# All low halves and block differences of an MLP's input and up-projection on VectorE

## The chip, the cores and the metric

The kernel runs on one core of a Trainium2 chip. The metric is device time in microseconds (us): the median of several executions. A profile of one further execution shows each engine's instructions: TensorE (PE, with its weight loads as PEld), VectorE (DVE), ScalarE (ACT), GpSimd (POOL) and SyncE (SP), which issues most DMAs.

## The reference

Two layers of a transformer-like backbone over 1024 latent and 256 context tokens of width 1024. Each layer normalises and modulates its input, runs three token mixers side by side (Fourier, mLSTM, attention), projects and adds, and then runs a squared-ReLU MLP. The change touches only the MLP's first half, and the place where the second layer's input is made:

```python
def sqrelu_mlp(h, w_up, w_down):
    return jnp.square(jax.nn.relu(h @ w_up)) @ w_down

for l in range(DEPTH):
    mod = (jax.nn.silu(c) @ w_mod[l] + b_mod[l])[:, None, :]
    sh1, sc1, ga1, sh2, sc2, ga2 = jnp.split(mod, 6, axis=-1)
    h = modulate(rmsnorm(x, g_norm1[l]), sh1, sc1)
    ...   # the three mixers
    x = x + ga1 * (jnp.concatenate([y_f, y_m, y_a], axis=-1) @ w_out[l])
    x = x + ga2 * sqrelu_mlp(modulate(rmsnorm(x, g_norm2[l]), sh2, sc2), w_up[l], w_down[l])
    ...   # in the first layer the same for the context tokens
```

`w_up` is 1024x4096 and all data are float32.

## The kernel before

**Numbers in two halves.** A float32 product is made from three TensorE passes: every operand is split into a high half, which ScalarE writes by a rounding copy (L147), and a low half, the source minus the high half (L148). The low half is a subtraction of two operands in SBUF, and VectorE or GpSimd makes it. `mm3` (L134 to L144) then issues high times high, high times low and low times high.

**Who makes the low half** is set by short patterns. `lo_` steps through a pattern's letters with one counter for all patterns of a layer (G is GpSimd, V is VectorE):

```python
def lo_(pat, c=[0]):
    c[0] += 1
    return G if pat[c[0] % len(pat)] == "G" else V
```

`LF` is for the low halves of the MLP's input and, at the end of the first layer, of the second layer's input; `UL` for those of the up-projection's weights; `UA` for the additions and subtractions on those weights (L1262); `FA` for those on the input (L1351); `DA` and `DL` for the down-projection.

**The up-projection** is a 2x2 block product after Strassen and Winograd, with seven products in place of eight. The latent input, 1024 tokens by 1024 channels, is cut in four; its block sums and differences S1 to S4 are made once for a layer (L1351 and the `split` calls around it). I call that stretch the build: it begins with the eight scalings L1190 of the second token block, which wait for that block's norm, and takes both token blocks in turn. The weights come as 16 pairs of column groups. For each pair, `up_pair` makes four differences (L1262), splits up to eight weight blocks, runs the products and adds up the results from PSUM (L1295 and L1313 to L1326). The first pairs' two products that need only the first token block (three pairs in the first layer, eight in the second) run during the build, so that TensorE has something to do. Split weight blocks (tiles `c` and `x`) have eight places in turn.

**Beside it, in the first layer,** VectorE computes the modulation of the second layer: 192 multiply-and-sum instructions (L235), each on a 256 KB piece of `w_mt`, two for each piece. The pieces land in three buffers (`wf`), which also hold results on their way to memory.

**The order of the work** on each engine is fixed when the program is built: a scheduler goes through the instructions with a cost of its own for each and writes one list for each engine, which that engine then works through strictly in order. Where another engine makes an instruction, the lists come out otherwise.

Of the kernel before, what the change touches and what calls it, by code (L numbers as in the profile page):

```python
# [29 lines left out]
PK0 = (1, 2, 4, 5, 7)  # L30
PK1 = (4, 5, 6)
PO = (7, 4, 0, 1, 5, 2, 3, 6)
UA = "GGV"
UL = "GGV"
FA = "V"
LF = "GV"
DA = "V"
DL = "VVVG"
RQ = "MAAV"
# [24 lines left out]
def build(tc, A, out, dbg=None):  # L64
# [81 lines left out]
    def split(dst, src, hi=None, lo=None):  # L146
        (hi or S).activation(dst[0], src, AF.Copy) if (hi is None or hi is S) else hi.tensor_copy(dst[0], src)  # L147
        (lo or G).tensor_tensor(dst[1], src, f32(dst[0]), ALU.subtract)  # L148
# [279 lines left out]
    for l in range(2):  # L428
# [752 lines left out]
# [4 lines that stand above are left out]
        def raw(l_, i_, b, h=None, R=None):  # L1185
            n, w = BLK[b][1:]
            R = rstd_bcast(ss[b], n, D, wk, pst, "t") if R is None else R
            for k in (0, 4, 1, 5, 2, 6, 3, 7):
                x = xT[b][:, k]
                hk["raw"] = V.scalar_tensor_tensor(x, x, Gm[l_][i_][:, w, k:k + 1], R[:, :n], ALU.mult, ALU.mult)  # L1190
                sh = modT[l_][:, w, 24 * i_ + k:24 * i_ + k + 1]
                S.activation(x, x, AF.Identity, bias=sh)
                if h is not None:
                    split((h[:, 0, k], h[:, 1, k]), x, lo=lo_(LF))
                yield k

        def form(b):
            h = h_tile(b)
            for k in raw(l, 1, b):
                split((h[:, 0, k], h[:, 1, k]), xT[b][:, k], lo=lo_(LF))  # L1200
            return h
# [27 lines left out]
        def rtile():  # L1229
            i = nslot[1] = (nslot[1] + 1) % len(rslot)  # L1230
            return T(wk, [128, 1024], tag="r2") if rslot[i] is None else rslot[i]

        def csplit(src, pat, c=None):
            c = ctile() if c is None else c
            split((c[:, 0], c[:, 1]), src, lo=lo_(pat))
            return c

        def prod(ps, c, h, first, last, n=512):
            for k in range(4):
                sl = slice(128 * k, 128 * k + 128)  # L1240
                mm3(ps, c[:, 0, sl], c[:, 1, sl], h[k][0][:, :n], h[k][1][:, :n], first and k == 0, last and k == 3)
# [11 lines left out]
        def P_(tag="p"):  # L1253
            return T(*((wk, [128, 512]) if tag == "p" else (ring, [128, 512])), tag=tag)
# [6 lines left out]
        def up_pair(p, a, b):  # L1261
            add = lambda *x: lo_(UA).tensor_tensor(*x)  # L1262
            ra = rtile()
# [13 lines left out]
            def pr_(c, h):  # L1277
                ps = mmt()
                prod(ps, c, H[h], True, True)
                return ps  # L1280

            if a:
                c11 = csplit(B11, UL)
                ps = pr_(c11, "A11")
# [4 lines left out]
                if cxa:  # L1289
                    psc = mmt()  # L1290
                    prod(psc[:, :256], c11, cx[:4], True, False, 256)
                c21 = csplit(B21, UL)
                ps = pr_(c21, "A12")
# [3 lines left out]
                if cxa:  # L1297
                    prod(psc[:, :256], c21, cx[4:], False, True, 256)
                    c12 = csplit(B12, UL)
            if b and not a and ctx_all:  # L1300
                p1s[p] = P_()
                nc.sync.dma_start(p1s[p], dp1[p])
            if b or cxa:
                c22 = csplit(B22, UL)
            if b:
# [3 lines left out]
                add(B22, B22, B11, ALU.subtract)  # L1309
                ps = pr_(csplit(B22, UL), "S2")  # L1310
                tg = "p"
                u2 = P_(tg)
                V.tensor_tensor(u2, ps, p1s[p], ALU.add)  # L1313
                add(B21, B21, B22, ALU.subtract)
                ps = pr_(csplit(B12, UL), "S3")
                u3 = P_(tg)
# [29 lines left out]
        for k in raw(l, 1, 1):  # L1346
# [4 lines left out]
            add = lambda *x: lo_(FA).tensor_tensor(*x)  # L1351
            split(H["A22"][i], r22, lo=lo_(LF))
            add(r22, r21, r22, ALU.add)
            add(r21, r11, r21, ALU.subtract)
            add(r11, r22, r11, ALU.subtract)
            split(H["S2"][i], r11, lo=lo_(LF))
            add(r12, r12, r11, ALU.subtract)
            split(H["S3"][i], r21, lo=lo_(LF))
            split(H["S1"][i], r22, lo=lo_(LF))
            split(H["S4"][i], r12, lo=lo_(LF))  # L1360
# [341 lines left out]
```

## Time and profile before

| | before |
|---|---|
| median of 3 executions | 3067.19 us (3059.11 to 3071.19) |
| the profiled execution | 3061.46 us, span 3059.7 us |
| TensorE busy | 2848.2 us, 93% |
| VectorE busy | 2012.7 us, 66% |
| ScalarE busy | 1177.9 us, 38% |
| GpSimd busy | 1062.4 us, 35% |
| mean granted TensorE clock | 0.955 |

The span runs from the first to the last instruction; the profiled execution's own time is 1.8 us longer. Busy shares are means over stages with different limits, so the windows, one for each stage, say more: the builds lie near 820 to 901 us and 2357 to 2438 us, the steady parts of the up-projections near 908 to 1257 us and 2440 to 2694 us, and the passage from the first layer to the second near 1640 to 1760 us.

### The profile page before, as it was taken

How to read it: one execution, taken by the hardware profiler on the slowest of the kernel's cores; microseconds unless marked ns; L12 is line 12 of the kernel's file. 1: busy time of each engine (PE TensorE's matmuls, PEld its weight loads, DVE VectorE, ACT ScalarE, POOL GpSimd, SP SyncE). 2: the span in 40 equal slices, each digit the busy share in tenths (PEclk: the TensorE clock that was granted, in tenths of full speed). 3: DMA queues.
4: the chain of work that ended last, by engine and by line, in shares of the span. 5: the costliest groups of instructions: out<-in, count | busy, mean ns of one | idle time of the engine just before them, and what ended most of it. 6: DMA issues, size and time to landing. Idle time of an engine off the chain costs nothing.

```text
span 3059.7 us, 40746 instructions
## 1 busy us (share of the span) xinstructions
PE 2848.2 (93%) x14320; PEld 2344.3 (77%) x14320; DVE 2012.7 (66%) x3742; ACT 1177.9 (38%) x2283; POOL 1062.4 (35%) x945
## 2 busy tenths in 40 slices
PE   7998998999989999999999999898999899989996
PEld 6887866657768888888887787876767688868885
DVE  7769568642488767777787527457633854478887
ACT  3322244443343333233344432244433543434444
POOL 4212234111364444221225333233123665513334
PEclk7999999999989999999999999899999899999998
DMA  6514576223335544732121212465134343353321
GB/s 238 161 56 136 145 170 165 72 88 112 111 128 196 168 159 156 281 111 94 58 90 38 109 40 87 123 152 138 55 115 140 117 153 106 110 196 97 106 88 55
DMA packets 277872, 376.45 MB, mean 123 GB/s; under 512 B 63396, under 2 KB 154468, under 8 KB 276004
## 3 DMA queue, kind: packets, MB, share of 16 engines
q1 hardware_dynamic: 274788, 366.51, 38.4%
q0 software_dynamic: 576, 4.20, 0.4%
q10 hardware_dynamic: 2304, 3.15, 0.3%
q8 instruction: 113, 1.85, 0.3%
q14 instruction: 91, 0.75, 0.1%
HBM read 283.74 MB, written 90.02 MB: 122 GB/s over the span
## 4 chain that ended last, share of the span: by engine, by line
PE 61%; DVE 18%; DMA 8%; issue 6%; POOL 3%; ACT 2%; SPq 0%; DVEq 0%; POOLq 0%; ACTq 0%
PE mm L138 10%; PE mm L143 8%; PE mm L144 8%; PE v L1141 4%; PE mm L135 4%; PE mm L136 4%; PE mm L134 3%; DVE ac L677 2%; DVE A L148 2%; DVE junk L235 2%; PE mm L1466 2%; PE mm L140 2%; PE mm L141 2%; PE t L1466 2%; DMA gt<-in_w_mt 2%
## 5 line engine op out<-in xcount | busy, mean ns | idle before, releaser
L138 PE MATMUL mm<-A,wr 128*128 128x512 f32 (+1 forms) x840 | 315.1, 378 | 18.6 <-ACT rb L673 9.8
L135 PE MATMUL mm<-A 128*128 128x512 f32 (+1 forms) x654 | 251.1, 389 | 13.6 <-DVE A L148 11.3
L136 PE MATMUL mm<-A 128*128 128x512 f32 (+1 forms) x654 | 242.8, 387 | 0.3 <-DVE A L148 0.3
L134 PE MATMUL mm<-A 128*128 128x512 f32 (+1 forms) x654 | 237.3, 387 | 5.7 <-ACT A L147 5.7
L148 POOL TENSOR_TENSOR wr<-wf,wr 128x512 fp32r<-128x512 f32 x88 | 123.1, 1407 | 246.3 <-ACT wr L147 235.3
L143 PE MATMUL mm<-A,wr 128*128 128x512 f32 (+1 forms) x520 | 194.5, 375 | 7.9 <-DVE A L148 4.3
L138 PEld LDWEIGHTS mm<-A,wr 128*128 128x128 f32 x840 | 162.4, 194 | 49.8 <-ACT rb L673 11.3
L1141 PE MATMUL v<-PT,Vt 128*97 128x512 f32 (+1 forms) x336 | 180.4, 622 | 14.0 <-ACT PT L1140 13.6
L144 PE MATMUL mm<-A,wr 128*128 128x512 f32 (+1 forms) x520 | 193.2, 372 | 0.0
L138 PE MATMUL mm<-A,c 128*128 128x512 f32 (+1 forms) x520 | 184.4, 356 | 5.8 <-ACT c L147 3.6
L143 PE MATMUL mm<-A,c 128*128 128x512 f32 (+1 forms) x520 | 184.9, 356 | 3.3 <-DVE A L148 2.5
L144 PE MATMUL mm<-A,c 128*128 128x512 f32 (+1 forms) x520 | 183.9, 354 | 1.2 <-DVE c L148 1.2
L235 DVE SCALAR_TENSOR_TENSOR junk<-wf,t 128x512 bf16<-128x512 f32 x192 | 131.3, 684 | 67.7 <-DMA wf<-in_w_mt 64.1
L147 ACT ACTIVATE A<-wr 128x512 fp32r<-128x512 f32 x188 | 114.2, 625 | 148.3 <-PE mm L135 59.2
L147 ACT ACTIVATE A<-A 128x512 fp32r<-128x512 f32 x174 | 106.9, 625 | 158.5 <-PE mm L135 86.0
L148 DVE TENSOR_TENSOR A<-wr,A 128x512 fp32r<-128x512 f32 x146 | 131.0, 909 | 43.4 <-ACT A L147 29.0
L1140 ACT ACTIVATE PT<-s 128x512 f32<-128x512 f32 (+1 forms) x168 | 97.6, 583 | 159.2 <-PE s L144 157.4
L135 PEld LDWEIGHTS mm<-A 128*128 128x128 f32 x654 | 123.4, 189 | 42.5 <-DVE A L148 15.0
L134 PEld LDWEIGHTS mm<-A 128*128 128x128 f32 x654 | 122.7, 188 | 31.1 <-ACT A L147 6.9
L136 PEld LDWEIGHTS mm<-A 128*128 128x128 f32 x654 | 123.6, 189 | 24.8 <-DVE A L148 0.7
L138 PE MATMUL mm<-wr,A 128*128 128x256 f32 x464 | 134.1, 289 | 6.9 <-ACT rb L673 4.7
L148 POOL TENSOR_TENSOR A<-wr,A 128x512 fp32r<-128x512 f32 x42 | 75.8, 1809 | 177.9 <-ACT A L147 149.8
(504 smaller groups left out, 8274.0 us busy)
## 6 DMA issues: line engine op xcount, KB each, us to landing
wf<-in_w_mt SPq DMA_DIRECT2D x96, 256.0 KB
x<-in_w_up SPq DMA_DIRECT2D x40, 512.0 KB
r<-in_w_up SPq DMA_DIRECT2D x38, 512.0 KB
wr<-in_w_dn SPq DMA_DIRECT2D x36, 512.0 KB
gt<-in_w_mt SPq DMA_DIRECT2D x64, 256.0 KB
da<-wf SPq DMA_DIRECT2D x64, 256.0 KB
da<-p SPq DMA_DIRECT2D x64, 256.0 KB
wf<-in_w_in SPq DMA_DIRECT2D x56, 256.0 KB
```

Of the source, the lines that this page charges most:

```text
L134: PE.matmul(ps, lh, rh, start=first, stop=False, skip_group_check=True)
L135: PE.matmul(ps, lh, rl, start=False, stop=False, skip_group_check=True)
L136: PE.matmul(ps, ll, rh, start=False, stop=last, skip_group_check=True)
L138: PE.matmul(ps, lh, rh, start=first, stop=False)
L143: PE.matmul(ps, lh, rl, start=False, stop=False)
L144: PE.matmul(ps, ll, rh, start=False, stop=last)
L147: (hi or S).activation(dst[0], src, AF.Copy) if (hi is None or hi is S) else hi.tensor_copy(dst[0], src)
L148: (lo or G).tensor_tensor(dst[1], src, f32(dst[0]), ALU.subtract)
L235: V.scalar_tensor_tensor(junk, f, 1.0, cb[w], ALU.mult, ALU.mult, accum_out=(ga, modT[l])[kh][:, w, j:j + 1])
L1140: S.activation(PT[:, :nq], ps[:, :nq], AF.Exp, scale=scale)
L1141: PE.matmul(po[:97, :nq], Vt[kt // 2][:, kt % 2, h % 2], PT[:, :nq], start=i == 0, stop=i == len(kts) - 1)
L1466: PE.matmul(o, blk[f"B{h + 1}{q + 1}"][k][:, 128 * jj:128 * jj + 128], f[:, k, 256 * h:256 * h + 256], start=h + k == 0, stop=h * k == 3)
```

## The change

Three patterns lose their G, so that every instruction under them goes to VectorE. `FA` had none.

```diff
-UA = "GGV"
-UL = "GGV"
+UA = "V"
+UL = "V"
 FA = "V"
-LF = "GV"
+LF = "V"
 DA = "V"
 DL = "VVVG"
```

What is computed is the same. The lists of the engines change. On VectorE, in the middle of the first layer's build, before: `x_` are the blocks being added and subtracted, `A_` and `wr_` the low halves of S1 to S4, `c_` those of weights, `wf_` results.

```order
L1351 TENSOR_TENSOR x_1563_7126<-x_1563_7126 128x512
L148 TENSOR_TENSOR wr_8026<-x_1563_7126,wr_8026 128x512
L1351 TENSOR_TENSOR x_1563_7126<-x_1563_7126 128x512
L1351 TENSOR_TENSOR x_1479_6740<-x_1563_7126,x_1479_6740 128x512
L148 TENSOR_TENSOR A_1674_8025<-x_1479_6740,A_1674_8025 128x512
L1251 SCALAR_TENSOR_TENSOR wf_8180<-mm_8104,wf_8180 128x512
```

The same place in VectorE's list after the change:

```order
L1351 TENSOR_TENSOR x_1563_7126<-x_1563_7126 128x512
L148 TENSOR_TENSOR c_8289<-r_1705_8222,c_8289 128x512
L148 TENSOR_TENSOR wr_8026<-x_1563_7126,wr_8026 128x512
L1351 TENSOR_TENSOR x_1479_6740<-x_1479_6740 128x512
L148 TENSOR_TENSOR wr_8030<-x_1563_7126,wr_8030 128x512
L1251 SCALAR_TENSOR_TENSOR wf_8180<-mm_8104,wf_8180 128x512
```

The low halves `c_8289` and `wr_8030`, which stood in GpSimd's list, now stand between VectorE's differences.

In the steady part of the first layer's up-projection, one stretch of VectorE's list before: `junk_` are the products for the modulation, each pair with its piece `wf_`, and `x_1716` the low half of a weight block.

```order
L1251 SCALAR_TENSOR_TENSOR wf_9916<-mm_9745,wf_9916 128x512
L235 SCALAR_TENSOR_TENSOR junk_9922,ga_8449<-wf_9920,t_8450 128x512
L235 SCALAR_TENSOR_TENSOR junk_9924,ga_8449<-wf_9920,t_8455 128x512
L148 TENSOR_TENSOR x_1716_8341<-r_2049_10196,x_1716_8341 128x512
L235 SCALAR_TENSOR_TENSOR junk_9938,mod_7_67<-wf_9936,t_9926 128x512
L235 SCALAR_TENSOR_TENSOR junk_9940,mod_7_67<-wf_9936,t_9931 128x512
L235 SCALAR_TENSOR_TENSOR junk_9944,mod_7_67<-wf_9942,t_9926 128x512
```

From the same result `wf_9916` on, after:

```order
L1251 SCALAR_TENSOR_TENSOR wf_9916<-mm_9745,wf_9916 128x512
L148 TENSOR_TENSOR c_10230<-r_2049_10196,c_10230 128x512
L235 SCALAR_TENSOR_TENSOR junk_9922,ga_8449<-wf_9920,t_8450 128x512
L235 SCALAR_TENSOR_TENSOR junk_9924,ga_8449<-wf_9920,t_8455 128x512
L1313 TENSOR_TENSOR p_10063<-mm_10050,p_9977 128x512
L148 TENSOR_TENSOR c_10263<-r_2050_10198,c_10263 128x512
L1262 TENSOR_TENSOR r_2050_10198<-r_2050_10198 128x512
L1317 TENSOR_TENSOR p_10081<-mm_10068,p_10063 128x512
L148 TENSOR_TENSOR x_1716_8341<-r_2050_10198,x_1716_8341 128x512
L1318 TENSOR_TENSOR p_10063<-mm_10031,p_10063 128x512
L235 SCALAR_TENSOR_TENSOR junk_9938,mod_7_67<-wf_9936,t_9926 128x512
```

Between the products on piece `wf_9920` and those on `wf_9936` there stood one low half; now there stand the sums of the next pair, two low halves and a difference.

## Rows read from the trace of the kernel before

**Rows 1.** The page: engine busy us (share of the span) xinstructions

```profile
PE 2848.2 (93%) x14320; PEld 2344.3 (77%) x14320; DVE 2012.7 (66%) x3742; ACT 1177.9 (38%) x2283; POOL 1062.4 (35%) x945
```

**Rows 2.** Windows: stretch and its length, busy us (xinstructions), clock, DMA

```profile
core 0: us, PE busy (x) PEld busy (x) DVE busy (x) ACT busy (x) POOL busy (x), PEclk, DMA share, GB/s
819.00:856.00 37.00, 29.71 (x147) 25.47 (x147) 28.16 (x58) 23.09 (x46) 17.45 (x16) 0.91 0.35 114
856.00:901.00 45.00, 32.40 (x174) 26.16 (x172) 44.93 (x44) 24.67 (x44) 30.78 (x20) 0.85 0.34 111
908.00:1257.00 349.00, 347.36 (x1815) 297.53 (x1814) 263.06 (x591) 120.82 (x209) 150.35 (x112) 1.00 0.53 172
...
2390.30:2437.70 47.40, 33.52 (x127) 24.60 (x126) 47.37 (x49) 27.35 (x49) 30.70 (x19) 0.82 0.33 111
2440.00:2694.00 254.00, 254.00 (x1090) 204.66 (x1089) 123.38 (x170) 100.39 (x165) 135.38 (x100) 1.00 0.37 124
```

**Rows 3.** TensorE's waits, 819 to 905 us: us in total, times, longest

```profile
PE mm L144 <- DVE c L148: 5.7, 2, 5.4
PE t L201 <- DVE rb_y L187: 4.8, 1, 4.8
```

**Rows 4.** TensorE's waits, 2350 to 2450 us

```profile
PE mm L138 <- ACT s L147: 8.4, 1, 8.4
```

**Rows 5.** Windows, TensorE alone, at the ends of the builds

```profile
880.00:905.00 25.00, 13.86 (x41) 0.66 0.40 137
2410.00:2438.00 28.00, 14.12 (x44) 0.70 0.38 131
2420.00:2430.00 10.00, 1.25 (x3) 0.50 0.20 59
```

**Rows 6.** VectorE in order of time, first build: start, us, instruction

```profile
855.89 5.35 DVE L1190 SCALAR_TENSOR_TENSOR x<-x,G,t 128x512 f32<-128x512 f32 x8
...
861.87 1.67 DVE L1351 TENSOR_TENSOR x<-x 128x512 f32<-128x512 f32 x1
863.47 0.68 DVE L1295 TENSOR_TENSOR wf<-mm,p 128x512 f32<-128x512 f32 x1
...
866.50 1.79 DVE L148 TENSOR_TENSOR A<-x,A 128x512 fp32r<-128x512 f32 x1
```

**Rows 7.** GpSimd in order of time, the same moments

```profile
861.53 1.47 POOL L148 TENSOR_TENSOR c<-r,c 128x512 fp32r<-128x512 f32 x1 [4.38 <-ACT c L147]
862.95 1.75 POOL L148 TENSOR_TENSOR A<-x,A 128x512 fp32r<-128x512 f32 x1
865.98 1.76 POOL L148 TENSOR_TENSOR A<-x,A 128x512 fp32r<-128x512 f32 x1 [1.27 <-DVE x L1351]
...
902.19 4.36 POOL L1262 TENSOR_TENSOR x<-x 128x512 f32<-128x512 f32 x3
906.50 1.28 POOL L148 TENSOR_TENSOR c<-x,c 128x512 fp32r<-128x512 f32 x1
```

**Rows 8.** VectorE in order of time, steady part of the first layer

```profile
1012.98 0.69 DVE L1318 TENSOR_TENSOR p<-mm,p 128x512 f32<-128x512 f32 x1
1013.59 0.69 DVE L148 TENSOR_TENSOR x<-r,x 128x512 fp32r<-128x512 f32 x1
1014.20 0.68 DVE L1320 TENSOR_TENSOR p<-mm,p 128x512 f32<-128x512 f32 x1
```

**Rows 9.** Windows, GpSimd's instructions of line L148 alone

```profile
819.00:856.00 37.00, 13.67 (x13) 0.91 0.35 114
856.00:901.00 45.00, 26.26 (x17) 0.85 0.34 111
```

**Rows 10.** VectorE by line, 908 to 1257 us: busy us, mean ns

```profile
L1251 DVE SCALAR_TENSOR_TENSOR wf<-wf 128x512 f32<-128x512 f32 x13 | 14.8, 1136 | 0.7 <-ACT wf L1250 0.7
L148 DVE TENSOR_TENSOR x<-x,x 128x512 fp32r<-128x512 f32 x18 | 13.6, 756 | 0.7 <-ACT x L147 0.7
L1248 DVE SCALAR_TENSOR_TENSOR p<-p 128x512 f32<-128x512 f32 x15 | 11.8, 784 | 0.0
...
L148 DVE TENSOR_TENSOR c<-x,c 128x512 fp32r<-128x512 f32 x9 | 7.4, 820 | 9.8 <-ACT c L147 9.8
```

**Rows 11.** VectorE's waits, 901 to 1258 us: us in total, times, longest

```profile
DVE junk L235 <- DMA wf<-in_w_mt: 64.1, 38, 4.1
```

**Rows 12.** Window: from the first layer to the second

```profile
1640.00:1720.00 80.00, 67.82 (x282) 53.31 (x281) 66.95 (x103) 46.12 (x90) 37.71 (x31) 0.91 0.22 85
```

**Rows 13.** TensorE's longest wait, 1640 to 1760 us

```profile
PE t L134 <- DVE x L1190: 4.0, 1, 4.0
```

## What is expected of the change

> **What bounds the kernel now.** I read the busy shares of the page first, then the stages by windows, then who ended TensorE's waits, then VectorE's and GpSimd's instructions in order of time. The shares say TensorE: 93% busy against VectorE's 66% and GpSimd's 35% [rows 1]. That is an average, so the windows decide. In the long middle of both up-projections TensorE never pauses: 347.4 of 349 us in the first layer, 254 of 254 in the second [rows 2]. What VectorE or GpSimd do there costs nothing as long as they keep ahead. In the stretch where the block differences of the MLP's input are made it is the reverse: VectorE is busy 44.9 of 45 us in the first layer and 47.4 of 47.4 in the second, while TensorE has 32.4 and 33.5 us of work [rows 2]. The waits agree: the longest of TensorE in the first layer is 5.4 us for a low half that VectorE makes, after 4.8 us for a norm chain on VectorE [rows 3]; in the second it is 8.4 us for ScalarE's copy of the last difference, which VectorE makes late [rows 4]. At the end of each stretch TensorE also runs slowly: 41 matmuls in 25 us at a granted clock of 0.66, 44 in 28 us at 0.70, of which 10 us at 0.50, that is 1.2 GHz, after it had stood idle [rows 5].
>
> **The change, part by part.** By the order, 292 subtractions leave GpSimd (950 instructions before, 658 after) and the same 292 stand on VectorE (3408, then 3700). The counts of the other engines are unchanged; TensorE's order shifts a little in the MLPs. The down-projection keeps its choices, because one counter serves all patterns and is still advanced once for each subtraction.
>
> Price of one moved subtraction: on VectorE undisturbed, neighbouring 128x512 subtractions start 0.60 us apart (1012.98, 1013.59, 1014.20) [rows 8]; on GpSimd one takes 1.3 us when it is alone and up to 1.8 in the build [rows 7]. But a GpSimd one isn't free for VectorE. The difference at 861.87 us and the low half at 866.50 us, both with two operands in SBUF, take 1.67 and 1.79 us beside GpSimd's subtractions, while the addition at 863.47, one operand of which is in PSUM, takes 0.68 us in the middle of one [rows 6, 7]. So a collision costs VectorE about 1.1 us, and the moved instruction 0.6.
> The Trainium skill, "SBUF — State Buffer", section "Who interferes with whom", says that a VectorE instruction with two SBUF inputs and a GpSimd one that reads SBUF take turns on a shared interface, the later one waiting for the whole of the other. The rows above agree, the PSUM case included. If every one of the 20 collided for 1.1 us, taking them away would give back 22 us for 12 spent, 10 us in that stretch, as an estimate from that rule; I go by the sum below instead.
>
> *The two build stretches.* First layer, 856 to 901 us: 44 VectorE and 20 GpSimd instructions, 17 of the latter low halves [rows 2, 9]; all 20 move. After: 64 x 0.60 us, and 0.06 us more for each of the eight scalings (eight take 5.35 us [rows 6]), is 38.9 us against 45.0: 6.1 us less. Second layer, 2390.3 to 2437.7 us: 49 and 19 instructions, 68 x 0.60 + 0.5 = 41.3 against 47.4: 6.1 us less. Together 12.2 us, if VectorE keeps never waiting. In the new order each low half stands close behind its difference, so a few will wait for ScalarE's high half (ScalarE is busy 24.7 and 27.4 us here [rows 2]); and in the second layer the last difference stands only a few places from the end, so that TensorE's 8.4 us wait shrinks less than the whole. I take 10 us of the 12.2. Bounds: nothing, if the waits for ScalarE eat it, and 12.2 plus what the clock gives back: 85 matmuls are busy 28.0 us [rows 5], at the undisturbed 254.0/1090 = 0.233 us [rows 2] it were 19.8, so 8.2 us more.
>
> *Before the first build, 819 to 856 us.* 13 low halves move [rows 9] onto an engine with 28.2 of 37 us busy [rows 2], part of that stretched by collisions; 13 x 0.60 = 7.8 fits into the 8.8 left. Nothing, between 4.8 us gained (the wait for the norm chain [rows 3] gone) and 4.8 lost (it doubles).
>
> *The steady up-projection, first layer.* 112 instructions move in 349 us [rows 2]. VectorE then has 263.1 + 112 x 0.60 = 330.3 us, less the collisions that end. These show in four groups as the excess over 0.69 us: 13 x 0.45, 18 x 0.07, 15 x 0.10, 9 x 0.13, 9.8 us [rows 10]. So 320.5 us, 92% of the stretch, with 28.5 us left. Queued there too are the products for the next layer's modulation (L235), 192 of them, in front of which VectorE stands 64.1 us waiting for their weights to land [rows 11]. If these waits stayed whole, 320.5 + 64.1 would be 35.6 us more than 349, and TensorE would pay that. I expect them to be filled: they come where VectorE goes through these products one behind the other with nothing else queued. In the order before, 114 of the 192 follow directly on another; in the order after 46, since the low halves now stand between. By that proportion 64.1 x 46/114 = 25.9 us of waiting remain, less than the 28.5. Cost: 0, between 0 and 35.6.
>
> *The steady up-projection, second layer.* 123.4 + 100 x 0.60 = 183.4 of 254 us [rows 2], without those products: 0. Some 70 us of VectorE's time stay idle there, so that what comes late is caught up.
>
> *From the first layer to the second, 1640 to 1720 us.* VectorE is busy 67.0 of 80 us and TensorE waits 4.0 us for its scalings [rows 12, 13]. Eight low halves move there and four just behind, all after that wait; at 0.6 us or less each that is under 5 us more on VectorE, and GpSimd keeps its share of the down-projection, so collisions go on. 0, within 3 us either way.
>
> **Sum.** The profiled execution took 3061.5 us, 3059.7 of it span. 10 us less is 3051.5. It stands 5.7 us under the median of 3067.2, so the forecast in the median's terms is 3057 us.
>
> **Rivals.** *More than the forecast:* the builds give all: 12.2 us, the clock's 8.2 and the norm chain's 4.8, 25 us, so 3042 us. For it: VectorE had no gap in either stretch [rows 2], and the slow matmuls stand right behind the idle time. Against: TensorE's order still begins the first full weight block with the product that needs the last differences, so some idle time stays, and with it some low clock.
> *Slower: VectorE becomes the bound in the first layer's steady stretch.* Low halves stand behind a product whose weights have not landed; the three buffers of these weights are also those in which results wait for their way out, and each is now held longer, since its two products no longer stand together. It decides as soon as more than 28.5 of the 64.1 us remain. With all of it: 35.6 less the builds' 10, 25.6 us more, so 3093 us. For it: 92% load and an engine that works strictly in order. Against: eight split weight blocks have room, each the work of 12 matmuls, 2.8 us at 0.233, so that a wait of 4.1 us (the longest [rows 11]) can pass unseen; and the fewer neighbours counted above.
> The Trainium skill, "Perfetto Trace Analysis", section "Optimizing Scalar/DVE Operations", would have work taken off VectorE when it is saturated, to GpSimd even, while warning that the shared read port may spoil that: the first half speaks against this change at 92%, the second for it.
> *Nothing happens:* the stretch is held by the chain difference, ScalarE's copy, low half, matmul, not by the number of VectorE's instructions; it then ends when it did, 3067 us. Against: VectorE's idle time there is nought.
>
> **How the numbers follow.** Forecast (2 to 15 us gained) 0.46, more 0.25, slower 0.22, nothing 0.07. Half a per cent is 15 us, about what a measurement of this kernel can tell from no change. The forecast and the nothing lie within it, as does a mild form of the slower case (0.01); of the forecast 0.02 goes over the line. So 0.27 faster, 0.52 same, 0.21 slower. The range runs from 3040 (the greater gain, and a little for the median's scatter) to 3088 (most of the slower case); the likeliest case alone would have 3050 to 3067.
>
> **What would show it.** In the profile after, the steps are right if GpSimd is nearly empty in both up-projections; VectorE's subtractions in the builds are 0.6 to 0.7 us and none 1.7; the time from the first scaling of the second block (855.9 and 2390.3 us before) to TensorE's steady running is about 6 and 4 us shorter; TensorE is over 99% busy in the steady stretches, with VectorE near 90% in the first layer and its waits for the modulation's weights down to some 25 us. The prediction is wrong if TensorE shows gaps there released by VectorE's low halves or additions, with VectorE waiting for those weights in front of them, or if VectorE in the builds now waits for ScalarE as long as it was held up before.

## The result, and the profile after

The changed kernel takes 3047.94 us, median of 6 executions (3044.08 to 3051.81), against 3063.22 us for the kernel before, run beside it (also 6, 3058.50 to 3071.19). The ratio is 0.9947, with a 95% interval of 0.9931 to 0.9962: 15.3 us faster by the medians, 11.6 to 21 by the interval. The profiled execution took 3047.78 us, 13.7 us less than the one of before. The forecast was 3057 us. The gain of 0.53% is about the half per cent that the prediction took for the least that can be told from no change; the interval leaves no change out, and when the same kernel ran again, below, the gain was 0.66%.

The page of the kernel after; it answers to [rows 1], with the same columns.

```profile
PE 2841.8 (93%) x14320; PEld 2343.2 (77%) x14320; DVE 2112.7 (69%) x4034; ACT 1179.0 (39%) x2283; POOL 667.8 (22%) x653
```

GpSimd lost 292 instructions and 394.6 us of busy time. VectorE gained the same 292 instructions, but only 100.0 us. At 0.60 us each they are 175 us of work, so VectorE's other instructions became some 75 us cheaper, as an estimate.

To see where the time came from I cut out the two stretches that the change is about. Each runs from the first scaling L1190 of a layer's MLP to its first down-projection combination (L1445, on VectorE), and so covers the first token block, the build and the long middle. TensorE alone, the kernel before (length of the stretch, busy us, granted clock):

```profile
818.40:1279.00 460.60, 439.02 (x2270) 0.97 0.52 173
2361.50:2706.80 345.30, 327.11 (x1383) 0.97 0.40 133
```

The kernel after:

```profile
823.60:1275.80 452.20, 437.97 (x2282) 0.98 0.53 177
2355.30:2693.80 338.50, 326.37 (x1382) 0.98 0.41 136
```

The stretches are 8.4 and 6.8 us shorter, 15.2 together. Length minus busy time is TensorE's idle time: 21.6 and 18.2 us before, 14.2 and 12.1 after, 13.4 less together. The other 1.8 us is busy time that became shorter at a somewhat higher clock. The two layers gave about equally. Outside the stretches the changed kernel took 1.5 us more: 5.2 more before the first one, in code that the change leaves alone, 3.0 less between the two, where twelve moved low halves lie, and 0.7 less after the second. Differences of this size stand between executions of one kernel: of the changed kernel's two profiled executions one reaches the first stretch at 823.6 and the other at 814.1 us, while their two stretches together are 15.2 and 16.2 us shorter than before.

Windows of the kernel after, answering to [rows 2], [rows 5] and [rows 12]. The first layer up to the build, its build and its long middle come first, then the same of the second layer. Then come the passage from layer to layer, and the ends of the two builds.

```profile
core 0: us, PE busy (x) PEld busy (x) DVE busy (x) ACT busy (x) POOL busy (x), PEclk, DMA share, GB/s
823.60:860.10 36.50, 30.64 (x155) 25.51 (x154) 30.62 (x70) 23.07 (x46) 5.33 (x3) 0.91 0.36 116
860.10:903.50 43.40, 35.04 (x194) 29.61 (x193) 43.34 (x73) 26.51 (x47) 0.00 (x0) 0.88 0.47 157
903.50:1252.80 349.30, 349.30 (x1824) 299.31 (x1823) 311.21 (x701) 121.41 (x208) 0.00 (x0) 1.00 0.52 172
2355.30:2380.40 25.10, 20.55 (x86) 15.98 (x85) 21.46 (x43) 17.82 (x32) 1.58 (x1) 0.86 0.41 124
2380.40:2429.00 48.60, 42.26 (x169) 32.50 (x168) 48.60 (x81) 29.70 (x54) 0.00 (x0) 0.93 0.42 139
2429.00:2681.00 252.00, 252.00 (x1082) 203.16 (x1081) 167.93 (x265) 100.68 (x164) 0.00 (x0) 1.00 0.37 125
1640.00:1720.00 80.00, 66.28 (x289) 53.70 (x288) 63.69 (x110) 45.26 (x88) 32.23 (x22) 0.91 0.21 80
878.00:903.00 25.00, 16.64 (x81) 13.07 (x80) 24.93 (x43) 11.99 (x21) 0.00 (x0) 0.80 0.49 169
2402.00:2430.00 28.00, 21.66 (x81) 15.99 (x80) 28.00 (x47) 14.23 (x26) 0.00 (x0) 0.88 0.49 166
```

The kernel before between the same marks, in the same order (of the first layer the front, that is the first token block, the build and the long middle; of the second the front and the build):

```profile
818.40:855.90 37.50, 30.21 (x152) 25.95 (x151) 28.66 (x58) 23.09 (x46) 17.34 (x16) 0.91 0.35 113
855.90:908.30 52.40, 39.76 (x200) 32.09 (x199) 46.80 (x46) 25.82 (x46) 37.59 (x24) 0.84 0.39 131
908.30:1257.00 348.70, 347.06 (x1813) 297.27 (x1813) 263.06 (x591) 120.82 (x209) 150.35 (x112) 1.00 0.53 172
2361.50:2390.30 28.80, 25.73 (x110) 20.05 (x109) 20.07 (x35) 19.11 (x34) 17.07 (x13) 0.94 0.44 139
2390.30:2440.20 49.90, 36.02 (x138) 26.60 (x137) 49.10 (x51) 28.37 (x51) 32.42 (x21) 0.83 0.35 116
```

Length minus TensorE's busy time says where its 13.4 us of idle time went: 4.3 in the first build (12.6 to 8.4), 7.5 in the second (13.9 to 6.3), 1.6 in the first layer's long middle (1.6 to none). The fronts cancel: 1.4 less in the first layer, 1.5 more in the second.

The reader is to see three things. GpSimd does nothing in the builds and the long middles. VectorE gets through 73 instructions in the first build's 43.4 us, where it did 46 in 52.4. And TensorE is still idle at the ends of the builds, but has 81 matmuls there at clocks of 0.80 and 0.88, in place of 41 and 44 at 0.66 and 0.70 [rows 5].

VectorE in order of time, first build, after, answering to [rows 6] (start, us, instruction):

```profile
866.59 0.69 DVE L1295 TENSOR_TENSOR wf<-mm,p 128x512 f32<-128x512 f32 x1
867.19 0.68 DVE L1351 TENSOR_TENSOR x<-x 128x512 f32<-128x512 f32 x1
867.79 0.69 DVE L148 TENSOR_TENSOR A<-x,A 128x512 fp32r<-128x512 f32 x1
868.39 0.69 DVE L1351 TENSOR_TENSOR x<-x,x 128x512 f32<-128x512 f32 x1
```

Every addition and subtraction of the two builds takes 0.68 to 0.70 us, and neighbours start 0.60 us apart; the 1.67 and 1.79 of [rows 6] are gone. TensorE's waits of the first layer's front and build and, below the dots, the second's, after (us in total, times, longest), answering to [rows 3] and [rows 4]:

```profile
PE mm L144 <- DVE c L148: 3.4, 2, 2.2
PE mm L138 <- ACT A L147: 2.9, 1, 2.9
PE mm L143 <- DVE x L148: 2.8, 1, 2.8
PE mm L138 <- ACT x L147: 2.3, 1, 2.3
...
PE mm L143 <- DVE s L148: 5.8, 2, 5.7
PE mm L143 <- DVE A L148: 2.4, 1, 2.4
```

The longest wait of the first build fell from 5.4 to 2.8 us (the 2.9 lies in the front), that of the second from 8.4 to 5.7, and the 4.8 us wait for the norm chain doesn't appear. VectorE's waits in the long middle of the first layer, after, answering to [rows 11]:

```profile
DVE junk L235 <- DMA wf<-in_w_mt: 31.1, 25, 5.4
```

### The profile page after: what moved, and what is told of

It is laid out like the page before. It is cut to its first block, busy times and chain, and to the rows that moved or that the text cites. A ratio compares the mean times of both kernels' runs of the same rounds, so it can differ in the third digit from the quotient of the medians.

```text
span 3046.0 us, 40618 instructions
## 1 busy us (share of the span) xinstructions
PE 2841.8 (93%) x14320; PEld 2343.2 (77%) x14320; DVE 2112.7 (69%) x4034; ACT 1179.0 (39%) x2283; POOL 667.8 (22%) x653
## 4 chain that ended last, share of the span: by engine, by line
PE 57%; DVE 19%; DMA 10%; issue 6%; POOL 3%; ACT 3%; SPq 0%; DVEq 0%; POOLq 0%; ACTq 0%
PE mm L138 9%; PE mm L143 7%; PE mm L144 7%; PE v L1141 4%; PE mm L135 4%; PE mm L136 4%; PE mm L134 3%; DVE junk L235 3%; DMA wf<-in_w_mt 2%; DVE A L148 2%; DVE ac L677 2%; PE mm L1466 2%; PE mm L140 2%; PE mm L141 2%; DMA gt<-in_w_mt 2%
## 5 line engine op out<-in xcount | busy, mean ns | idle before, releaser
L1141 PE MATMUL v<-PT,Vt 128*97 128x512 f32 (+1 forms) x336 | 178.1, 616 | 12.9 <-ACT PT L1140 12.6
L148 POOL TENSOR_TENSOR wr<-wf,wr 128x512 fp32r<-128x512 f32 x88 | 125.2, 1431 | 289.1 <-ACT wr L147 267.3
L148 DVE TENSOR_TENSOR A<-wr,A 128x512 fp32r<-128x512 f32 x146 | 128.8, 894 | 43.3 <-ACT A L147 29.0
L235 DVE SCALAR_TENSOR_TENSOR junk<-wf,t 128x512 bf16<-128x512 f32 x192 | 131.0, 682 | 32.8 <-DMA wf<-in_w_mt 31.1
L1140 ACT ACTIVATE PT<-s 128x512 f32<-128x512 f32 (+1 forms) x168 | 97.3, 583 | 134.1 <-PE s L144 133.7
L138 PE MATMUL mm<-wr,A 128*128 128x256 f32 x464 | 134.3, 290 | 6.6 <-ACT rb L673 4.7
L143 PE MATMUL mm<-wr,A 128*128 128x256 f32 x464 | 133.9, 289 | 0.0
```

Source lines behind the costliest of these rows:

```text
L138: PE.matmul(ps, lh, rh, start=first, stop=False)
L143: PE.matmul(ps, lh, rl, start=False, stop=False)
L235: V.scalar_tensor_tensor(junk, f, 1.0, cb[w], ALU.mult, ALU.mult, accum_out=(ga, modT[l])[kh][:, w, j:j + 1])
L1140: S.activation(PT[:, :nq], ps[:, :nq], AF.Exp, scale=scale)
L1141: PE.matmul(po[:97, :nq], Vt[kt // 2][:, kt % 2, h % 2], PT[:, :nq], start=i == 0, stop=i == len(kts) - 1)
```

## The experiments

Each kernel ran beside the kernel before on the same chip; the ratios, with their 95% intervals, are to those runs, whose medians were 3055.67 us (the first four kernels), 3056.68 (the next four) and 3058.68 (the last two).

**Each half of the change alone.** The input's low halves alone:

```diff
-LF = "GV"
+LF = "V"
```

> Only the low halves of the MLP's input (and of the next layer's input) go to VectorE; weights and their differences stay as before. Theory (collisions in the builds): about half of the 20 and 19 GpSimd instructions of the builds go, so 5 to 9 us less than before. Rival (the gain is the list of TensorE, drawn up anew): anything from 0 to the whole 15 us, without regard to how many collisions go. The profile decides: VectorE's 1.7 us instructions in the builds should be about halved in number.

Measured: 3046.72 us, ratio 0.9969 (0.9958 to 0.9980), 9.5 us. The weights' differences and low halves alone:

```diff
-UA = "GGV"
-UL = "GGV"
+UA = "V"
+UL = "V"
```

> Only the weights' low halves and differences go to VectorE; the input's low halves stay half on GpSimd. Theory: the other half of the builds' collisions goes, 5 to 9 us less than before, and e1 and e2 together give about the change's 15 us. VectorE's load in the first layer's steady stretch is that of the change (311 of 349 us), so if that stretch costs anything, this run shows it and e1 doesn't.

Measured: 3046.35 us, ratio 0.9965 (0.9953 to 0.9978), 10.7 us, with 12 executions that scatter from 3035.85 to 3056.32. Either half is worth about 10 us, and 9.5 + 10.7 is about what the whole gives (16.2 and 20.2 us by its two ratios, of 3056). So it does not need the last collision to be gone before anything is won. In the one profiled execution of each the two stretches are 6.1 and 5.3 us shorter with the inputs' half, and 6.2 and 1.0 with the weights' half, which works mostly in the first layer by this. VectorE's instructions of over 1.2 us, from the second block's first scaling to the last low half of the input's blocks, number 16 and 13 in the builds of the kernel before and 6 and 7 with the inputs' half: about halved, as expected. But both runs have another order of instructions too, and it counts. With the inputs' half, the last of these low halves of the second layer comes 45.2 us after the second block's first scaling, 43.5 in the kernel before, and yet that stretch became 5.3 us shorter. So the rival, TensorE's list drawn up anew, is not ruled out for this half.

**GpSimd's reads put back, without its work.** To the changed kernel, GpSimd subtractions are added behind the splits of the build, 20 in each layer, behind those of A22, S1, S2, S3 and S4 (the diff shows one). Their result goes to a buffer that nobody reads. The written order on TensorE, VectorE, ScalarE and SyncE is the same, instruction for instruction, as in the changed kernel.

```diff
+            dmy = T(wk, [128, 512], tag="dmy")
-            split(H["S2"][i], r11, lo=lo_(LF))
+            split(H["S2"][i], r11, lo=lo_(LF)); decoy(G, dmy, f32(H["S2"][i][0]))
...
+def decoy(G, dmy, src):
+    G.tensor_tensor(dmy, src, src, ALU.subtract)
```

> The changed kernel, and after each of the 20 splits in a layer's build one GpSimd subtraction that reads the high half just written and writes a tile that nobody uses. The lists of TensorE, VectorE, ScalarE and SyncE are those of the changed kernel. Theory (VectorE is held up by GpSimd's reads): VectorE's two-operand instructions in the builds take 1.7 us again, 10 to 20 us more in each layer, so 20 to 40 us above the changed kernel and slower than before. Rival (the gain is shorter low halves and the new lists): as the changed kernel, within 4 us.

Measured: 3065.41 us, ratio 1.0032 (1.0021 to 1.0043): slower than the kernel before. The second kernel has the same places, but there GpSimd reads one column and writes the buffer three times:

```diff
-    G.tensor_tensor(dmy, src, src, ALU.subtract)
+    G.tensor_tensor(dmy[:, :1], src[:, :1], src[:, :1], ALU.subtract)
+    for _ in range(3):
+        G.memset(dmy, 0.0)
```

> As the run with reading decoys, but each decoy reads one column and then only writes (three fills of 128x512), so that GpSimd is about as busy. Theory, by the part of it on reading (VectorE waits only for GpSimd's reads): within 5 us of the changed kernel. Rival (any GpSimd work beside VectorE slows it): as the reading decoys.

Measured: 3041.14 us, ratio 0.9938 (0.9917 to 0.9958), as the change itself. The two kernels are 24.3 us apart. The first build with the reads; the window, with the columns above:

```profile
851.30:908.70 57.40, 36.50 (x190) 29.83 (x189) 57.40 (x73) 26.57 (x47) 29.41 (x20) 0.76 0.35 119
```

And three of VectorE's groups in it (line, instruction, count, then busy us and mean ns):

```profile
L148 DVE TENSOR_TENSOR wr<-x,wr 128x512 fp32r<-128x512 f32 x10 | 9.6, 981 | 0.0
...
L1351 DVE TENSOR_TENSOR x<-x,x 128x512 f32<-128x512 f32 x8 | 7.9, 996 | 0.0
...
L1295 DVE TENSOR_TENSOR wf<-mm,p 128x512 f32<-128x512 f32 x2 | 1.4, 680 | 0.0
```

The same window with the writes:

```profile
853.40:896.70 43.30, 35.43 (x195) 29.76 (x194) 43.22 (x72) 26.52 (x47) 30.47 (x28) 0.88 0.46 158
```

And the groups:

```profile
L148 DVE TENSOR_TENSOR wr<-x,wr 128x512 fp32r<-128x512 f32 x10 | 6.5, 677 | 0.0
...
L1351 DVE TENSOR_TENSOR x<-x,x 128x512 f32<-128x512 f32 x8 | 5.3, 677 | 0.0
...
L1295 DVE TENSOR_TENSOR wf<-mm,p 128x512 f32<-128x512 f32 x2 | 1.4, 677 | 0.0
```

GpSimd is busy 29.4 and 30.5 us, though not with the same: of the 30.5 us, 11.0 are 21 buffer writes and 19.6 are seven reads of one column, which are held up themselves (last section). VectorE has the same instructions in the same order. With reads they fill 57.4 us, with writes 43.2. The stretching falls on instructions with two operands in SBUF (981 and 996 ns in the groups shown, against 677), and not on L1295, which reads PSUM (680 against 677). 14.1 us over 20 reads is 0.7 us a read. The second layer shows the same: the two stretches of the up-projection are 14.7 and 14.9 us longer with reads than with writes. So at one order of instructions, and with no low half of GpSimd's in either kernel, GpSimd's reads alone stretch VectorE's work and cost the kernel 24 us.

One count sets all these kernels side by side, one profiled execution each. From the second block's first scaling to the last low half of the input's blocks, first layer / second layer:

| kernel | length, us | VectorE's instructions | GpSimd's | length less 0.60 us for each of VectorE's |
|---|---|---|---|---|
| before | 43.5 / 43.5 | 44 / 47 | 19 / 18 | 17.1 / 15.3 |
| inputs alone | 40.6 / 45.2 | 54 / 60 | 9 / 10 | 8.2 / 9.2 |
| weights alone | 39.0 / 43.5 | 49 / 55 | 10 / 10 | 9.6 / 10.5 |
| the change | 35.4 / 40.9 | 59 / 68 | 0 / 0 | 0.0 / 0.1 |
| with reads | 49.7 / 55.1 | 59 / 68 | 20 / 20 | 14.3 / 14.3 |
| with writes | 35.4 / 40.8 | 59 / 68 | 17 / 17 | 0.0 / 0.0 |

The last column is what GpSimd's work costs VectorE: 0.7 to 1.05 us for each of its instructions that reads 128x512, and nothing for the buffer writes and one-column reads. How much of the change's own 15 us is this, and how much its new order, no run separates, since the change brings both. The Trainium skill, "SBUF — State Buffer", section "Who interferes with whom", states that a VectorE instruction with two SBUF inputs contends with a GpSimd instruction that reads SBUF and not with one that only writes it; this pair agrees in both halves, at 57.4 against 43.2 us.

**How near the slower rival was.** The change once more, as the base for this set of runs:

> The changed kernel once more, as the measure for the other runs of this call: 0.9947 of the kernel before, within 0.0015 (13 to 20 us less).

Measured: 3034.14 us (3033.81 to 3035.32), ratio 0.9934 (0.9917 to 0.9951). Then with 52 additions on VectorE whose results nobody needs, four in each of 13 pairs of the first layer's long middle. The scheduler writes the lists anew around them.

```diff
-                out_(u3, 2, RQ[2])
+                out_(u3, 2, RQ[2]); [V.tensor_tensor(dmy, f32(c22[:, 0]), f32(c22[:, 0]), ALU.add) for _ in range(4 if l == 0 and a else 0)]
```

> The changed kernel with four idle VectorE additions of 0.6 us (they read a split weight block and write a tile that nobody uses) in each of the 13 full pairs of the first layer's up-projection: 52, 31 us more work for VectorE, which has 311 of 349 us there and waits 31 us for the modulation's weights. Theory (those waits are filled by whatever else is queued): 0 to 6 us above the changed kernel, the waits down to some 10 us. Rival of the prediction (VectorE becomes the bound at 28.5 us of remaining waits): the new work is paid in full, 20 to 31 us more.

Measured: 3049.69 us, ratio 0.9987 (0.9973 to 1.0000): 15.6 us more than the change. Neither theory has the size. Window of the long middle with the extra load:

```profile
900.00:1258.00 358.00, 348.72 (x1810) 296.43 (x1809) 332.08 (x728) 123.32 (x205) 0.00 (x0) 1.00 0.48 165
```

And in the change run again:

```profile
900.00:1258.00 358.00, 358.00 (x1874) 306.96 (x1874) 316.73 (x706) 128.99 (x223) 4.10 (x3) 1.00 0.54 182
```

TensorE has 9.3 us of idle time in the first and none in the second. Its waits there with the load:

```profile
PE mm L138 <- ACT p L1286: 5.5, 4, 3.5
PE mm L138 <- DVE wf L1295: 3.7, 7, 0.9
```

And VectorE's:

```profile
DVE junk L235 <- DMA wf<-in_w_mt: 8.5, 9, 1.6
DVE c L148 <- ACT c L147: 5.9, 11, 1.4
DVE x L148 <- ACT x L147: 4.2, 5, 1.3
```

So the waits for modulation weights were filled from 29.2 us (in the change run again) to 8.5, as the theory has it. But TensorE stalled before they were used up, on ScalarE's copies of PSUM results (L1286) and on VectorE's sums from PSUM (L1295), and VectorE took on new short waits for ScalarE. Of 31 us of load (52 x 0.60) half was paid by the medians; in the profiled executions the first layer's stretch alone grew by 20.2 us, from 449.7 to 469.9, the lower edge of the rival, and the code between the stretches took 5.8 less. VectorE as the bound is a real mechanism here. By this one load it is some 11 to 16 us of load away, as an estimate.

**The same reasoning elsewhere in the MLP.** Two edits on top of the change that take more two-operand reads apart: the down-projection's low halves from GpSimd, and the squares of the first product pair's results, which VectorE multiplies from two SBUF operands, to ScalarE.

```diff
-DL = "VVVG"
+DL = "V"
```

> The changed kernel with the down-projection's low halves on VectorE too (there one in four is GpSimd's). TensorE is busy 376 of 382 and 275 of 290 us there, so if collisions matter only where TensorE waits for VectorE, little is to be had: 2 to 6 us less, from the starts of the down-projections, where TensorE waits 6.4 us for a low half and 5.6 us for VectorE's sums. Rival: VectorE, busy 251 of 290 us there, becomes the bound: 5 to 15 us more.

Measured: 3028.18 us, ratio 0.9909 (0.9894 to 0.9925), 6.0 us below the change by the medians: the upper edge of what was expected. The two intervals overlap, but the slowest of its 6 executions (3030.34) is faster than the fastest of the change's 4 (3033.81).

```diff
-RQ = "MAAV"
+RQ = "AAAV"
```

> The changed kernel with the squares of the first product pair's result (16 in each layer) on ScalarE in place of VectorE. VectorE is busy without a gap in the builds, ScalarE 26.5 of 43 and 29.7 of 49 us. Theory (the builds last as long as VectorE has instructions): 2 squares less in the first layer's build and some 7 in the second's, 0.6 us each, so 3 to 6 us less than the changed kernel. Rival (the builds are now held by the chain difference, copy, low half): 0, or a few us more, since ScalarE makes the copies that low halves wait for.

Measured: 3032.35 us, ratio 0.9923 (0.9905 to 0.9941), 1.8 us below the change. The interval of the change run again covers it, so by the time this one is not told from nothing. In the trace the theory held where it was about: by the count of the table the builds took 34.8 and 37.3 us, against 35.4 and 40.9 in the change, 4.2 us less together. Both together:

> The changed kernel with both steps: the down-projection's low halves on VectorE and the first pair's squares on ScalarE. If their gains (7.6 and 1.8 us by the medians against the changed kernel of the same call) lie in different stretches, they add: 8 to 12 us less than the changed kernel, 0.989 to 0.991 of the kernel before. If they take the same idle time, as the better of the two, 0.991.

Measured: 3025.92 us, ratio 0.9885 (0.9865 to 0.9906), which does not tell adding up from the better of the two. (The 7.6 us in the expectation is by the ratios; by the medians it is 6.0.) Last, 100 low halves on GpSimd that `wunit` makes, of weights loaded outside the MLP's first half:

```diff
-        split((r[:, 0], r[:, 1]), f, lo=V if wcnt[0] < wcnt[1] and wcnt[0] % 2 else G)
+        split((r[:, 0], r[:, 1]), f, lo=V)
```

> As e8, and the low halves of the input projection's weights (wunit, some 90 on GpSimd) on VectorE too. Theory (a move pays where TensorE waits for VectorE and VectorE collides): TensorE's waits there are for ScalarE's copies and a norm chain, VectorE has 96.7 of 145 and 102.4 of 135 us of work: within 4 us of e8. Rival (each collision taken away pays): 10 us or more less than e8.

Measured: 3008.33 us, ratio 0.9834 (0.9814 to 0.9854), the best version here: 50 us under the kernel before. I had expected at most 4 us from this step, and it gave 17.6 by the medians (15.6 by the ratios); the rival's 10 or more has the size. From the first L1140 to the first L1190, the first layer's mixers, the time fell from 435.1 to 423.8 us. A window of 120 us there, without the last edit:

```profile
620.00:740.00 120.00, 106.61 (x421) 69.79 (x420) 43.34 (x79) 44.48 (x86) 18.57 (x14) 0.96 0.29 89
```

And with it:

```profile
620.00:740.00 120.00, 110.33 (x496) 76.11 (x496) 48.88 (x94) 45.02 (x87) 5.11 (x4) 1.00 0.32 103
```

VectorE is busy 43 us of 120, so its share is no guide here; TensorE gets through 496 matmuls in the window, where it did 421. The order on all engines differs between the two kernels as well, and I have not separated the order from the collisions. What this last gain is made of stays open.

## Why the prediction was right or wrong

**What bounds the kernel: right.** VectorE in the builds, TensorE in the long middles, both as [rows 2] had them. With 20 reads put back VectorE's 57.4 of 57.4 us set the end; with none it still does (43.34 of 43.40, 48.60 of 48.60 us), only sooner.

**The collision: right in kind, too large in size.** I took 1.1 us from single hits of 1.67 and 1.79 us. Averaged over a build, a read of GpSimd cost VectorE 0.7 us in the experiment (14.1 over 20). In the kernel before, by the prediction's own way of counting, it cost (44.93 - 44 x 0.60 - 0.5) / 20 = 0.9 us. The sum did not use the 1.1; its 6.1 us for each build are these 0.9 less the 0.60 of the moved instruction, some 20 times.

**The builds, 10 of 12.2 us: nearly right together, not layer by layer.** TensorE's idle time in the builds fell by 11.8 us, close to the whole 12.2, but by 4.3 and 7.5 and not by twice 6.1. VectorE's part became 8.1 and 2.7 us shorter to the input's last low half (the table above), because the new lists put 15 and 21 more instructions on VectorE there, where 19 and 18 of GpSimd's fell away. In the second layer the front, which the sum left out, became 3.7 us shorter as well. The sign that I had named, that TensorE runs steadily some 6 and 4 us sooner after the second block's first scaling, came out as 9 and 6 (43.6 to 34.3 and 47.0 to 40.9 us, to the end of its last pause of 0.15 us or more). Of the two reasons for taking 2.2 us off, the first was wrong: VectorE shows no wait for ScalarE's high halves in either build. The second held: the 8.4 us wait shrank to 5.7 and not to nothing.

**Why the forecast lay 9 us too high.** The two stretches gave 15.2 us where I had 10: the builds 1.8 more than taken, the long middle 1.6 where I had nothing, and the clock 1.8, which I had put wholly into the "more" rival at 8.2. The other 4 of the 9 us against 3047.9 come from the base: the kernel before was 3063.2 us beside the changed one, not the 3067.2 that I started from.

**Before the first build, 0 within 4.8: held.** That stretch took 36.5 us, 1 us less than before from the same marks, and the wait for the norm chain is gone; other waits took its place, so that TensorE's idle time there fell by 1.4 us and not by 4.8. VectorE is busy 30.6 of 36.5 us, 70 instructions where it had 58.

**Steady first layer, 0: no cost, right with some luck.** TensorE is 349.3 of 349.3 us busy; its one wait there before, 1.6 us for a modulation product (L235) on VectorE, is gone, a gain that I had not counted. The waits for the weights came to 31.1 us where I said 25.9, and by my own threshold of 28.5 that would have decided for the slower rival. It didn't, since VectorE's busy time was 311.2 and not 320.5: the four groups of [rows 10] showed 9.8 us of collisions, and 263.1 + 112 x 0.60 - 311.2 = 19.1 had gone. So two misses cancelled: more waits were left, and more collisions ended, than I had counted. The proportion by neighbours in the order was a fair guide. The test with more load puts the margin at some 11 to 16 us.

**Steady second layer and the passage, 0: right.** 252.0 of 252.0 us; between the layers TensorE's wait for L1190 is 4.0 us as before [rows 13], and VectorE 63.7 us busy rather than 67.0.

**The rivals.** Of "more than the forecast" the clock's part came to a quarter of its 8.2, and of the norm chain's 4.8 the front of the first layer shows about 1 us. "Slower" did not occur, but its mechanism was there to be provoked. "Nothing happens" is refuted: the number of VectorE's instructions, and what each takes, set the end of the input's low halves (the table), even if the order moves TensorE's time too.

## What to carry to other kernels

Before an instruction goes to a helper engine, ask what its reads cost the engine that it relieves: here 0.7 to 1.05 us of VectorE for each GpSimd read of 128x512 among two-operand instructions, against 0.60 us to do the work itself. Count the price in the stretch where that engine is the bound, not over the span. And look where the added load lands: of the waits it is to fill, only part was usable (11 to 16 of 29 us here, as an estimate).

## What the runs showed that I had not expected

The collision runs the other way too. In the kernel with the writes, GpSimd's groups in the first build are these:

```profile
L1705 POOL TENSOR_TENSOR dmy<-wr 128x1 f32<-128x1 f32 x3 | 15.0, 4991 | 0.2
L1707 POOL MEMSET dmy<- 128x512 f32 x21 | 11.0, 526 | 1.2
L1705 POOL TENSOR_TENSOR dmy<-A 128x1 f32<-128x1 f32 x4 | 4.6, 1140 | 27.5 <-ACT A L147 27.4
```

A read of one column took 0.19 us beside VectorE's scalings, which read one operand from PSUM (at 857.21 us), and 5.0 us on the mean of three among VectorE's back-to-back subtractions, the time of about eight of them and not of one. The buffer writes beside them kept 0.53 us. A busy VectorE can therefore hold up a small GpSimd step by microseconds, which the mixers, where GpSimd has such steps, may also feel; that was not tried.
